# Instance normalization on one core: 24 of 32 units joined in pairs, longer rows for their loads, column halves for their stores

## The chip, the core and the metric

The kernel runs on one core of a Trainium2 chip. The core has five engines that run side by side, each with its own instruction stream: TensorE (PE, matrix products), VectorE (DVE), ScalarE (ACT), GpSimd (POOL) and SyncE (SP). Data move between HBM (the chip's main memory) and SBUF (the on-chip memory with 128 partitions) by 16 DMA engines, which are fed from queues; a queue belongs to the engine that issues the transfer. The metric is the device time of one execution in microseconds (us).

## The reference

```python
B, G, C_per_g, H, W = 4, 8, 16, 256, 256
mu = x.mean(axis=(3, 4), keepdims=True)
var = ((x - mu) ** 2).mean(axis=(3, 4), keepdims=True)
x_norm = (x - mu) / np.sqrt(var + 1e-5)
out = x_norm * gamma[None, :, :, None, None]
```

There are 512 channels of 65,536 float32 numbers. Each is normalized by its own mean and variance and multiplied by its gamma. The input is 134.2 MB and the output as much; both are read or written once.

## The kernel before, in words

The input is cut into `U` = 32 units of 4 MB (16 channels each). A unit lies in SBUF as 128 partitions of `F` = 8192 numbers (32 KB), so that one channel takes `S` = 8 neighbouring partitions. Every partition's row is one run of 32 KB in HBM, and the rows of a unit follow each other without a gap.

There are `AHEAD` = 6 slots of 4 MB in SBUF. `load(u)` brings unit u into slot u % 6. The first six loads are issued at the start: units 1 and 3 by ACT, the others by SP. After that, the load of unit u + 6 stands in the program behind the store of unit u; it is issued by SP, which waits until that store has landed, since it writes the same slot.

For each unit, in order:

- VectorE sums each partition's row (L106) while ScalarE sums the squares (L107, whose elementwise result goes to `junk` and is not used).
- TensorE multiplies the two columns of sums by `navg` (L115), a 128x128 matrix that holds -1/65536 where two partitions belong to one channel. The result `ps` has minus the mean and minus the mean square, already spread over the channel's partitions.
- A short chain makes the scale: `nvar` (L116, VectorE), `std` (L120, ScalarE, a square root), `rstd` (L124, VectorE), and `scale` with gamma's column `g_col` (L126, VectorE).
- VectorE scales the unit in place (L135). For unit 0 ScalarE does the last three eighths (L132).
- ACT issues the store of the unit (L139), and then stands ready for the next unit's squares.

Ahead of the loop, POOL writes a small piece of the output (`touch`), loads gamma and builds `navg`; VectorE repeats gamma eight times along a row (L80), eight small products turn that into columns (L85), and VectorE copies them to `g_col` (L91).

The order of instructions on each engine is the order of the program. Both DMA queues that matter are in this order too: q1 is fed by SP (30 loads), q10 by ACT (2 loads and all 32 stores).

Of the kernel before, what the change touches and what calls it, by code (L numbers as in the profile page):

```python
# [1 line left out]

# [4 lines left out]

F32 = mybir.dt.float32
U8 = mybir.dt.uint8
ALU = mybir.AluOpType  # L10
ACTF = mybir.ActivationFunctionType
AX = mybir.AxisListType


@with_exitstack
def kernel(
    ctx: ExitStack,
    tc: tile.TileContext,
    x: bass.AP,
    gamma: bass.AP,  # L20
    out: bass.AP,
):
    nc = tc.nc
    B, G, C, H, W = x.shape
    P = nc.NUM_PARTITIONS
    HW = H * W
    n_ch = B * G * C
    S = 8
    K = P // S
    F = HW // S  # L30
    U = n_ch // K
    NG = (G * C) // K
    AHEAD = 6
    assert HW % S == 0 and (G * C) % K == 0

    xv = x.rearrange("b g c h w -> (b g c h w)").rearrange("(u p f) -> u p f", p=P, f=F)
    ov = out.rearrange("b g c h w -> (b g c h w)").rearrange("(u p f) -> u p f", p=P, f=F)
    gv = gamma.rearrange("g c -> (g c)")

    data = ctx.enter_context(tc.tile_pool(name="data", bufs=1))  # L40
    singles = ctx.enter_context(tc.tile_pool(name="singles", bufs=1))
    psum = ctx.enter_context(tc.tile_pool(name="psum", bufs=4, space=bass.MemoryType.PSUM))
    ctx.enter_context(tc.manual_schedule())

    slots = [data.tile([P, F], F32, name=f"xt{i}") for i in range(AHEAD)]

    def load(u, queue):
        queue.dma_start(out=slots[u % AHEAD][:], in_=xv[u])  # L48


    g_row = singles.tile([1, G * C], F32, name="g_row")
    touch = singles.tile([16, 128], F32, name="touch")
    nc.vector.memset(touch[:], 0.0)  # L53
    nc.gpsimd.dma_start(out=ov[0][0::S, 0:128], in_=touch[:])  # L54
    nc.gpsimd.dma_start(out=g_row[:], in_=gv[None, :])  # L55
    for u in range(AHEAD):
        load(u, nc.scalar if u in (1, 3) else nc.sync)

    eps_t = singles.tile([P, 1], F32, name="eps_t")
    nc.gpsimd.memset(eps_t[:], 1e-5)  # L60
    one = singles.tile([1, 1], F32, name="one")
    nc.gpsimd.memset(one[:], 1.0)
    navg = singles.tile([P, K, S], F32, name="navg")
    nc.gpsimd.memset(navg[:], -1.0 / HW)  # L64
    nc.gpsimd.affine_select(  # L65
        out=navg[:], in_=navg[:], pattern=[[-S, K], [0, S]], compare_op=ALU.is_ge,
        fill=0.0, base=0, channel_multiplier=1,
    )
    nc.gpsimd.affine_select(  # L69
        out=navg[:], in_=navg[:], pattern=[[S, K], [0, S]], compare_op=ALU.is_ge,  # L70
        fill=0.0, base=S - 1, channel_multiplier=-1,
    )
    navg_w = navg[:].rearrange("p k s -> p (k s)")
    root_eps = singles.tile([P, 1], F32, name="root_eps")
    nc.scalar.activation(out=root_eps[:], in_=eps_t[:], func=ACTF.Sqrt)  # L75
    g_rep = singles.tile([1, NG, K, S], F32, name="g_rep")
    g_ps = psum.tile([P, NG], F32, name="g_ps", bufs=1)
    g_col = singles.tile([P, NG], F32, name="g_col")

    nc.vector.tensor_copy(  # L80
        out=g_rep[:],
        in_=g_row[:].rearrange("o (n k) -> o n k", n=NG).unsqueeze(3).to_broadcast([1, NG, K, S]),
    )
    for n in range(NG):
        nc.tensor.matmul(  # L85
            out=g_ps[:, n : n + 1],
            lhsT=g_rep[:, n].rearrange("o k s -> o (k s)"),
            rhs=one[:],
            start=True, stop=True,
        )  # L90
    nc.vector.tensor_copy(out=g_col[:], in_=g_ps[:])  # L91

    junk = singles.tile([P, F], U8, name="junk")

    st = singles.tile([P, U, 2], F32, name="st")
    nvar = singles.tile([P, U], F32, name="nvar")
    std = singles.tile([P, U], F32, name="std")
    rstd = singles.tile([P, U], F32, name="rstd")
    scale = singles.tile([P, U], F32, name="scale")

    shift = singles.tile([P, 1], F32, name="shift")

    squares = []
    for u in range(U):
        t = slots[u % AHEAD]
        nc.vector.reduce_sum(out=st[:, u, 0:1], in_=t[:], axis=AX.X)  # L106
        square = nc.scalar.activation(  # L107
            out=junk[:], in_=t[:], func=ACTF.Square, accum_out=st[:, u, 1:2],
        )
        if u:  # L110

            tc.declare_no_dep(square.ins, squares[-1].ins, reason="junk, ordered by the root between")
        squares.append(square)
        ps = psum.tile([P, 2], F32, name="ps")
        nc.tensor.matmul(out=ps[:], lhsT=navg_w, rhs=st[:, u], start=True, stop=True)  # L115
        nc.vector.tensor_scalar(  # L116
            out=nvar[:, u : u + 1], in0=ps[:, 0:1], scalar1=ps[:, 0:1],
            scalar2=ps[:, 1:2], op0=ALU.mult, op1=ALU.add,
        )
        nc.scalar.activation(  # L120
            out=std[:, u : u + 1], in_=nvar[:, u : u + 1], func=ACTF.Sqrt,
            bias=eps_t[:], scale=-1.0,
        )
        nc.vector.reciprocal(out=rstd[:, u : u + 1], in_=std[:, u : u + 1])  # L124
        g = u % NG
        nc.vector.tensor_mul(  # L126
            out=scale[:, u : u + 1], in0=rstd[:, u : u + 1], in1=g_col[:, g : g + 1],
        )
        cut = F * 5 // 8 if u == 0 else F
        if cut < F:  # L130
            nc.vector.tensor_mul(out=shift[:], in0=ps[:, 0:1], in1=scale[:, u : u + 1])  # L131
            nc.scalar.activation(  # L132
                out=t[:, cut:], in_=t[:, cut:], func=ACTF.Identity, bias=shift[:], scale=scale[:, u : u + 1],
            )
        nc.vector.tensor_scalar(  # L135
            out=t[:, :cut], in0=t[:, :cut], scalar1=ps[:, 0:1], scalar2=scale[:, u : u + 1],
            op0=ALU.add, op1=ALU.mult,
        )
        nc.scalar.dma_start(out=ov[u], in_=t[:])  # L139
        if u + AHEAD < U:  # L140
            load(u + AHEAD, nc.sync)


# [1 line left out]
_INS = ['x', 'gamma']  # L145
_OUTS = [((4, 8, 16, 256, 256), 'float32')]


# [23 lines left out]
```

## Time and profile before

| | us |
|---|---|
| median of 3 runs | 626.83 (626.78 to 626.91) |
| span of the profiled execution, first to last instruction | 625.2 |
| VectorE busy | 441.8 |
| ScalarE busy | 241.8 |
| TensorE busy | 21.4 |

The trace gives the profiled execution's span; what the timed runs have on top of it is 1.6 us. A row of digits in the profile cuts the span in 40 equal slices and gives the busy share of each in tenths. "DMA" is the mean over the core's 16 DMA engines. A line of the groups names the code line, the engine, the operation, what it writes and reads, the shapes and the count; then the busy time in us and the mean in ns of one; then the engine's idle time just before these instructions and what ended it. "Chain of waits" is the chain of work that ended last, followed back from the last instruction. In it each unit at the start takes VectorE 14.93 us from one reduction to the next.

### The profile page before, as it was taken

How to read it: one execution, taken by the hardware profiler on the slowest of the kernel's cores; microseconds unless marked ns; L12 is line 12 of the kernel's file. 1: busy time of each engine (PE TensorE's matmuls, PEld its weight loads, DVE VectorE, ACT ScalarE, POOL GpSimd, SP SyncE). 2: the span in 40 equal slices, each digit the busy share in tenths (PEclk: the TensorE clock that was granted, in tenths of full speed). 3: DMA queues.
4: the chain of work that ended last, by engine and by line, in shares of the span. 5: the costliest groups of instructions: out<-in, count | busy, mean ns of one | idle time of the engine just before them, and what ended most of it. 6: DMA issues, size and time to landing. Idle time of an engine off the chain costs nothing.

```text
span 625.2 us, 635 instructions
## 1 busy us (share of the span) xinstructions
PE 21.4 (3%) x80; PEld 19.5 (3%) x80; DVE 441.8 (71%) x164; ACT 241.8 (39%) x99; POOL 2.4 (0%) x11
## 2 busy tenths in 40 slices
PE   0200000000000000000000000000000000000000
PEld 0200000000000000000000000000000000000000
DVE  0589999998776687666786767867668676687730
ACT  0464444444443244432344423444224442244400
POOL 1000000000000000000000000000000000000000
DMA  8999999999999999999999999999999999999998
GB/s 370 436 407 432 436 436 436 436 436 430 423 436 434 434 428 434 434 436 436 436 436 428 426 436 436 432 430 434 434 436 436 436 436 421 432 436 434 434 430 367
DMA packets 9282, 268.46 MB, mean 429 GB/s; under 512 B 1072, under 2 KB 1088, under 8 KB 1088
## 3 DMA queue, kind: packets, MB, share of 16 engines
q10 hardware_dynamic: 4896, 142.61, 52.9%
q1 hardware_dynamic: 4320, 125.83, 46.8%
q0 software_dynamic: 64, 0.01, 0.0%
q14 instruction: 2, 0.02, 0.0%
HBM read 134.22 MB, written 134.23 MB: 429 GB/s over the span
## 4 chain that ended last, share of the span: by engine, by line
another core or an unknown queue 61%; DMA 17%; DVE 15%; SPq 1%; PE 1%; issue 0%; ACT 0%
DMA xt<-in_x_dram 10%; DVE st L106 10%; DMA out_dram<-xt 8%; DVE xt L135 5%; SPq L48 1%; PE ps L115 1%; ACT std L120 0%; DVE nvar L116 0%; DVE rstd L124 0%; DVE scale L126 0%; DVE shift L131 0%
## 5 line engine op out<-in xcount | busy, mean ns | idle before, releaser
L106 DVE TENSOR_REDUCE st<-xt 128x1 f32<-128x8192 f32 x32 | 277.9, 8684 | 102.2 <-DMA xt<-in_x_dram 102.2
L107 ACT ACTIVATE junk<-xt 128x8192 uint8<-128x8192 f32 x32 | 225.0, 7030 | 272.0 <-DMA xt<-in_x_dram 233.8
L135 DVE TENSOR_SCALAR xt<-xt,ps,scale 128x8192 f32<-128x8192 f32 (+1 forms) x32 | 144.0, 4500 | 1.1
L120 ACT ACTIVATE std<-nvar,eps_t 128x1 f32<-128x1 f32 x32 | 9.4, 295 | 79.4 <-DVE nvar L116 79.4
L115 PE MATMUL ps<-st,navg 128*128 128x2 f32 x64 | 17.8, 348 | 557.3 <-DVE st L106 557.3
L115 PEld LDWEIGHTS ps<-st,navg 128*128 128x128 f32 x64 | 16.0, 310 | 559.1 <-issue 546.2
L116 DVE TENSOR_SCALAR nvar<-ps 128x1 f32<-128x1 f32 x32 | 9.2, 286 | 23.8 <-PE ps L115 23.8
L124 DVE RECIPROCAL rstd<-std 128x1 f32<-128x1 f32 x32 | 5.2, 163 | 11.6 <-ACT std L120 11.6
L80 DVE COPY g_rep<-g_row 1x1024 f32<-1x1024 f32 x1 | 0.7, 681 | 14.4 <-DMA g_row<-in_gamma_dram 14.4
L107 ACT ACTIVATION_READ_ACCUMULATOR junk<-xt 128x1 f32 x32 | 6.0, 186 | 0.0
L126 DVE TENSOR_TENSOR scale<-rstd,g_col 128x1 f32<-128x1 f32 x32 | 5.1, 158 | 1.1
L85 PE MATMUL g_ps<-one,g_rep 1*128 1x1 f32 x16 | 3.5, 347 | 16.3 <-DVE g_rep L80 16.3
L85 PEld LDWEIGHTS g_ps<-one,g_rep 1*128 1x128 f32 x16 | 3.5, 326 | 16.3 <-issue 16.3
L132 ACT ACTIVATE xt<-xt,shift,scale 128x3072 f32<-128x3072 f32 x1 | 2.9, 2947 | 0.7 <-DVE shift L131 0.7
L91 DVE COPY g_col<-g_ps 128x8 f32<-128x8 f32 x1 | 0.2, 167 | 3.7 <-PE g_ps L85 3.7
L75 ACT ACT_TABLE_LOAD x1 | 1.3, 1283 | 1.7 <-PEq L156 1.7
L53 DVE MEMSET touch<- 16x128 f32 x1 | 0.2, 165 | 0.9 <-PEq L156 0.9
L54 POOL DMA_DIRECT2D out_dram<-touch x1 | 0.6, 617 | 0.8 <-DVE touch L53 0.8
L55 POOL DMA_DIRECT2D g_row<-in_gamma_dram x1 | 0.5, 487 | 0.0
L65 POOL TENSOR_SCALAR_AFFINE_SELECT navg<-navg 128x128 f32<-128x128 f32 x1 | 0.4, 400 | 0.1
L69 POOL TENSOR_SCALAR_AFFINE_SELECT navg<-navg 128x128 f32<-128x128 f32 x1 | 0.4, 399 | 0.1
L64 POOL MEMSET navg<- 128x128 f32 x1 | 0.2, 230 | 0.0
(8 smaller groups left out, 1.0 us busy)
## 6 DMA issues: line engine op xcount, KB each, us to landing
out_dram<-xt ACTq DMA_DIRECT2D x32, 4096.0 KB, 62.5
xt<-in_x_dram SPq DMA_DIRECT2D x30, 4096.0 KB, 38.5
xt<-in_x_dram ACTq DMA_DIRECT2D x2, 4096.0 KB, 31.7
out_dram<-touch POOLq DMA_DIRECT2D x1, 8.0 KB, 9.3
g_row<-in_gamma_dram POOLq DMA_DIRECT2D x1, 0.5 KB, 13.5
```

The costliest lines, as they stand in the source:

```text
L48: queue.dma_start(out=slots[u % AHEAD][:], in_=xv[u])
L75: nc.scalar.activation(out=root_eps[:], in_=eps_t[:], func=ACTF.Sqrt)
L85: nc.tensor.matmul(out=g_ps[:, n : n + 1], lhsT=g_rep[:, n].rearrange("o k s -> o (k s)"), rhs=one[:], start=True, stop=True,)
L106: nc.vector.reduce_sum(out=st[:, u, 0:1], in_=t[:], axis=AX.X)
L107: square = nc.scalar.activation(out=junk[:], in_=t[:], func=ACTF.Square, accum_out=st[:, u, 1:2],)
L115: nc.tensor.matmul(out=ps[:], lhsT=navg_w, rhs=st[:, u], start=True, stop=True)
L116: nc.vector.tensor_scalar(out=nvar[:, u : u + 1], in0=ps[:, 0:1], scalar1=ps[:, 0:1], scalar2=ps[:, 1:2], op0=ALU.mult, op1=ALU.add,)
L120: nc.scalar.activation(out=std[:, u : u + 1], in_=nvar[:, u : u + 1], func=ACTF.Sqrt, bias=eps_t[:], scale=-1.0,)
L124: nc.vector.reciprocal(out=rstd[:, u : u + 1], in_=std[:, u : u + 1])
L126: nc.vector.tensor_mul(out=scale[:, u : u + 1], in0=rstd[:, u : u + 1], in1=g_col[:, g : g + 1],)
L132: nc.scalar.activation(out=t[:, cut:], in_=t[:, cut:], func=ACTF.Identity, bias=shift[:], scale=scale[:, u : u + 1],)
L135: nc.vector.tensor_scalar(out=t[:, :cut], in0=t[:, :cut], scalar1=ps[:, 0:1], scalar2=scale[:, u : u + 1], op0=ALU.add, op1=ALU.mult,)
```

## The change

24 of the 32 units (4 to 27) are joined in pairs to twelve units of 8 MB. A joined unit has 32 channels, a channel takes 4 partitions (`S` = 4), and a partition's row is one run of 64 KB in HBM. It is loaded by one DMA. It is stored by two, one for each half of the columns: rows of 32 KB that step 64 KB in HBM. The first four and the last four units stay at 4 MB. In the order of units there are now 20: four single, twelve joined, four single.

The six slots become three tiles of 8 MB; a single unit takes one half of such a tile, a joined unit a whole one. The first five loads (four single units, one joined) are issued at the start. A later load is issued when the stores of all data that it overwrites have landed, so a joined one waits for two stores.

The reductions and squares keep their shape, 128 x 8192, so a joined unit has two of each; two products accumulate in one `ps`, and there is one short chain for the whole unit. The scaling is done half by half, and each half's store is issued as soon as it is scaled. `navg` and `g_col` are made twice, for S = 8 and S = 4.

```diff
-    S = 8
-    AHEAD = 6
+    HALVES = 6
+    ENDS = 4
+    sizes = [1] * ENDS + [2] * ((n_half - 2 * ENDS) // 2) + [1] * ENDS
+    starts = [sum(sizes[:i]) for i in range(len(sizes))]
...
+    def rows(flat, u):
+        n = sizes[u] * P * F
+        lo = starts[u] * P * F
+        return flat[lo : lo + n].rearrange("(p f) -> p f", p=P)
...
-    slots = [data.tile([P, F], F32, name=f"xt{i}") for i in range(AHEAD)]
+    pairs = [data.tile([P, 2 * F], F32, name=f"xt{i}") for i in range(HALVES // 2)]
+
+    def home(u):
+        at = starts[u] % HALVES
+        return pairs[at // 2], (at % 2) * F
 
     def load(u, queue):
-        queue.dma_start(out=slots[u % AHEAD][:], in_=xv[u])
+        t, c = home(u)
+        src = rows(x_flat, u)
+        n = sizes[u] * F
+        step = n
+        for k in range(0, n, step):
+            queue.dma_start(out=t[:, c + k : c + k + step], in_=src[:, k : k + step])
...
-    for u in range(AHEAD):
+    first = [u for u in range(len(sizes)) if starts[u] + sizes[u] <= HALVES]
+    for u in first:
         load(u, nc.scalar if u in (1, 3) else nc.sync)
...
+    for S in (8, 4):
...
     for u in range(U):
-        t = slots[u % AHEAD]
-        nc.vector.reduce_sum(out=st[:, u, 0:1], in_=t[:], axis=AX.X)
-        square = nc.scalar.activation(
-            out=junk[:], in_=t[:], func=ACTF.Square, accum_out=st[:, u, 1:2],
-        )
+        t, c = home(u)
+        S = 8 // sizes[u]
+        halves = range(sizes[u])
+        for h in halves:
+            part = t[:, c + h * F : c + (h + 1) * F]
+            col = starts[u] + h
+            nc.vector.reduce_sum(out=st[:, col, 0:1], in_=part, axis=AX.X)
+            square = nc.scalar.activation(
+                out=junk[:], in_=part, func=ACTF.Square, accum_out=st[:, col, 1:2],
+            )
...
-        nc.tensor.matmul(out=ps[:], lhsT=navg_w, rhs=st[:, u], start=True, stop=True)
+        for h in halves:
+            nc.tensor.matmul(
+                out=ps[:], lhsT=navg[S], rhs=st[:, starts[u] + h],
+                start=h == 0, stop=h == sizes[u] - 1,
+            )
...
-        nc.vector.tensor_scalar(
-            out=t[:, :cut], in0=t[:, :cut], scalar1=ps[:, 0:1], scalar2=scale[:, u : u + 1],
-            op0=ALU.add, op1=ALU.mult,
-        )
-        nc.scalar.dma_start(out=ov[u], in_=t[:])
-        if u + AHEAD < U:
-            load(u + AHEAD, nc.sync)
+        dst = rows(o_flat, u)
+        step = F
+        for k in range(0, sizes[u] * F, step):
+            n = min(step, cut - k)
+            nc.vector.tensor_scalar(
+                out=t[:, c + k : c + k + n], in0=t[:, c + k : c + k + n], scalar1=ps[:, 0:1],
+                scalar2=scale[:, u : u + 1], op0=ALU.add, op1=ALU.mult,
+            )
+            nc.scalar.dma_start(out=dst[:, k : k + step], in_=t[:, c + k : c + k + step])
+
+        for v in range(len(first), U):
+            need = starts[v] + sizes[v] - HALVES
+            if starts[u] < need <= starts[u] + sizes[u]:
+                load(v, nc.sync)
```

More of the change, by code (lines that the diff above doesn't have):

```diff
@@ L26 @@
     HW = H * W
-    n_ch = B * G * C
-    S = 8
[L29 to L32, printed above, removed]
-    AHEAD = 6
-    assert HW % S == 0 and (G * C) % K == 0
-    xv = x.rearrange("b g c h w -> (b g c h w)").rearrange("(u p f) -> u p f", p=P, f=F)
-    ov = out.rearrange("b g c h w -> (b g c h w)").rearrange("(u p f) -> u p f", p=P, f=F)
+    F = 8192
+    HALVES = 6
+    n_half = (B * G * C * HW) // (P * F)
+    ENDS = 4
+    assert n_half * P * F == B * G * C * HW and HW % (2 * F) == 0
+    sizes = [1] * ENDS + [2] * ((n_half - 2 * ENDS) // 2) + [1] * ENDS
+    starts = [sum(sizes[:i]) for i in range(len(sizes))]
+    assert sum(sizes) == n_half
+    xf = x.rearrange("b g c h w -> (b g c h w)")
+    of = out.rearrange("b g c h w -> (b g c h w)")
     gv = gamma.rearrange("g c -> (g c)")
+    def rows(flat, u):
+        n = sizes[u] * P * F
+        lo = starts[u] * P * F
+        return flat[lo : lo + n].rearrange("(p f) -> p f", p=P)
     data = ctx.enter_context(tc.tile_pool(name="data", bufs=1))
@@ L43 @@
     ctx.enter_context(tc.manual_schedule())
-    slots = [data.tile([P, F], F32, name=f"xt{i}") for i in range(AHEAD)]
+    pairs = [data.tile([P, 2 * F], F32, name=f"xt{i}") for i in range(HALVES // 2)]
+    def home(u):
+        at = starts[u] % HALVES
+        return pairs[at // 2], (at % 2) * F
     def load(u, queue):
-        queue.dma_start(out=slots[u % AHEAD][:], in_=xv[u])
+        t, c = home(u)
[4 more added lines that the diff above has]
+            queue.dma_start(out=t[:, c + k : c + k + step], in_=src[:, k : k + step])
+    x_flat, o_flat = xf, of
     g_row = singles.tile([1, G * C], F32, name="g_row")
@@ L53 @@
     nc.vector.memset(touch[:], 0.0)
-    nc.gpsimd.dma_start(out=ov[0][0::S, 0:128], in_=touch[:])
+    nc.gpsimd.dma_start(out=rows(o_flat, 0)[0::8, 0:128], in_=touch[:])
     nc.gpsimd.dma_start(out=g_row[:], in_=gv[None, :])
-    for u in range(AHEAD):
+    first = [u for u in range(len(sizes)) if starts[u] + sizes[u] <= HALVES]
+    for u in first:
         load(u, nc.scalar if u in (1, 3) else nc.sync)
@@ L62 @@
     nc.gpsimd.memset(one[:], 1.0)
[L63 to L67, printed above, removed]
-    )
-    nc.gpsimd.affine_select(
-        out=navg[:], in_=navg[:], pattern=[[S, K], [0, S]], compare_op=ALU.is_ge,
-        fill=0.0, base=S - 1, channel_multiplier=-1,
-    )
-    navg_w = navg[:].rearrange("p k s -> p (k s)")
+    navg, g_col = {}, {}
@@ new lines @@
+    for S in (8, 4):
+        K = P // S
+        w = singles.tile([P, K, S], F32, name=f"navg{S}")
+        nc.gpsimd.memset(w[:], -1.0 / HW)
+        nc.gpsimd.affine_select(
+            out=w[:], in_=w[:], pattern=[[-S, K], [0, S]], compare_op=ALU.is_ge,
+            fill=0.0, base=0, channel_multiplier=1,
+        )
+        nc.gpsimd.affine_select(
+            out=w[:], in_=w[:], pattern=[[S, K], [0, S]], compare_op=ALU.is_ge,
+            fill=0.0, base=S - 1, channel_multiplier=-1,
+        )
+        navg[S] = w[:].rearrange("p k s -> p (k s)")
@@ L74 @@
     root_eps = singles.tile([P, 1], F32, name="root_eps")
     nc.scalar.activation(out=root_eps[:], in_=eps_t[:], func=ACTF.Sqrt)
[L76 to L89, printed above, removed]
-        )
@@ L91 @@
-    nc.vector.tensor_copy(out=g_col[:], in_=g_ps[:])
+    g_all = singles.tile([1, G * C * 8], F32, name="g_all")
+    for S in (8, 4):
+        K = P // S
+        n_g = (G * C) // K
+        g_rep = g_all[:, : G * C * S].rearrange("o (c s) -> o c s", s=S)
+        nc.vector.tensor_copy(
+            out=g_rep, in_=g_row[:].unsqueeze(2).to_broadcast([1, G * C, S]),
+        )
+        g_ps = psum.tile([P, n_g], F32, name=f"g_ps{S}", bufs=1)
+        g_col[S] = singles.tile([P, n_g], F32, name=f"g_col{S}")
+        for n in range(n_g):
+            nc.tensor.matmul(
+                out=g_ps[:, n : n + 1],
+                lhsT=g_all[:, n * P : (n + 1) * P],
+                rhs=one[:],
+                start=True, stop=True,
+            )
+        nc.vector.tensor_copy(out=g_col[S][:], in_=g_ps[:])
@@ L93 @@
     junk = singles.tile([P, F], U8, name="junk")
-    st = singles.tile([P, U, 2], F32, name="st")
+    U = len(sizes)
+    st = singles.tile([P, n_half, 2], F32, name="st")
     nvar = singles.tile([P, U], F32, name="nvar")
@@ L104 @@
     for u in range(U):
-        t = slots[u % AHEAD]
-        nc.vector.reduce_sum(out=st[:, u, 0:1], in_=t[:], axis=AX.X)
-        square = nc.scalar.activation(
-            out=junk[:], in_=t[:], func=ACTF.Square, accum_out=st[:, u, 1:2],
[L109 to L113, printed above, removed]
-        ps = psum.tile([P, 2], F32, name="ps")
-        nc.tensor.matmul(out=ps[:], lhsT=navg_w, rhs=st[:, u], start=True, stop=True)
+        t, c = home(u)
[7 more added lines that the diff above has]
+                out=junk[:], in_=part, func=ACTF.Square, accum_out=st[:, col, 1:2],
+            )
+            if squares and h == 0:
+                tc.declare_no_dep(square.ins, squares[-1].ins, reason="junk, ordered by the root between")
+            squares.append(square)
+        ps = psum.tile([P, 2], F32, name="ps")
+        for h in halves:
+            nc.tensor.matmul(
+                out=ps[:], lhsT=navg[S], rhs=st[:, starts[u] + h],
+                start=h == 0, stop=h == sizes[u] - 1,
+            )
         nc.vector.tensor_scalar(
```

14 lines of the change are left out of this document (8 added, 6 removed).

## The prediction

> **What bounds the kernel now.** I read the head of the page first, with its busy rows and its queue table.
>
> ```profile
> span 625.2 us, 635 instructions
> ...
> PE 21.4 (3%) x80; PEld 19.5 (3%) x80; DVE 441.8 (71%) x164; ACT 241.8 (39%) x99; POOL 2.4 (0%) x11
> ...
> DVE  0589999998776687666786767867668676687730
> ...
> DMA  8999999999999999999999999999999999999998
> ...
> q10 hardware_dynamic: 4896, 142.61, 52.9%
> q1 hardware_dynamic: 4320, 125.83, 46.8%
> ```
>
> No compute engine is full, but the two DMA queues together fill 52.9 + 46.8 = 99.7% of the time of all 16 DMA engines. The stretch view, asked for the middle of the run, says the same: DMA share 1.00 (the last but one number), at 433 GB/s.
>
> ```profile
> 110.00:540.00 430.00, 12.81 (x46) 11.50 (x46) 316.53 (x116) 170.60 (x69) 0.00 (x0) 1.00 1.00 433
> ```
>
> So the time is 268.46 MB at some 433 GB/s (620 us), plus about 1.8 us before the first byte, 1 to 2 us after the last, and little else. The waits of the SP queue (what, on what: us in total, times, longest) and the page's list of DMA issues (last number: us from issue to landing) show why no engine starves: loads wait for stores to free a slot, and stores stand in a line three deep (62.5 us to land, where 4.19 MB at 433 GB/s need 9.7 us alone and 19.4 us at half rate).
>
> ```profile
> SPq L48 <- DMA out_dram<-xt: 514.7, 26, 39.7
> ```
>
> ```profile
> out_dram<-xt ACTq DMA_DIRECT2D x32, 4096.0 KB, 62.5
> xt<-in_x_dram SPq DMA_DIRECT2D x30, 4096.0 KB, 38.5
> ```
>
> Last, the groups of instructions, for the durations:
>
> ```profile
> L106 DVE TENSOR_REDUCE st<-xt 128x1 f32<-128x8192 f32 x32 | 277.9, 8684 | 102.2 <-DMA xt<-in_x_dram 102.2
> L135 DVE TENSOR_SCALAR xt<-xt,ps,scale 128x8192 f32<-128x8192 f32 (+1 forms) x32 | 144.0, 4500 | 1.1
> L80 DVE COPY g_rep<-g_row 1x1024 f32<-1x1024 f32 x1 | 0.7, 681 | 14.4 <-DMA g_row<-in_gamma_dram 14.4
> L91 DVE COPY g_col<-g_ps 128x8 f32<-128x8 f32 x1 | 0.2, 167 | 3.7 <-PE g_ps L85 3.7
> ```
>
> VectorE idles 102.2 us ahead of its reductions, waiting for loads. It follows the DMAs, and its work is worth nothing unless it gets late enough to empty both queues.
>
> **The change, part by part.**
>
> *Fewer and longer packets.* In the queue table a packet is one row, plus one 4-byte semaphore write per DMA and engine: q1 has 30 loads x (128 + 16) = 4320. The change turns 24 x 128 = 3072 load rows of 32 KB into 1536 of 64 KB, so each of the 16 engines handles 96 fewer packets. The bytes stay. What is saved is the fixed cost of a packet, and no row shows a 64 KB packet. Its bounds come from the trace's packet records: 32 KB packets take 1213 ns nearly throughout, the 4-byte ones 9 ns. A packet that carries almost nothing bounds the fixed cost: 0 to 9 ns, so 96 packets save 0 to 0.86 us. I take the middle, 4.5 ns: 0.43 us. I do not reckon below nothing here, because a 64 KB row is the same run of bytes in both memories; a dearer row is the second rival.
>
> A rule of the Trainium skill ("DMA: Bandwidth & Descriptors", "Why small descriptors are slow") gives some 3 cycles a packet inside a DMA engine. At that page's 850 MHz this is 3.5 ns, an estimate by which the sum would be 0.34 us instead of 0.43.
>
> *Fewer DMAs.* 32 loads become 20, the stores stay 32: 12 fewer semaphore writes per engine at 9 ns, 0.11 us. Twelve issues on SP (0.33 us each in the chain of waits) go too, worth nothing: store packets keep the engines busy meanwhile.
>
> *Stores.* Same 32, same 32 KB rows, but 24 of them step 64 KB between rows in HBM. No row has that step. I take no cost, as the nearest row is the present store at a step of 32 KB, whose packets take the same 1213 ns as the loads'. The other end is in the second rival.
>
> *Compute per unit.* A joined unit has two reductions, then one chain instead of two, then two scalings: 2 x 8.68 + 0.57 x 2 (PE, now two accumulated products) + about 1.4 (nvar, std, rstd, scale and their gaps) + 2 x 4.55 = 29.0 us, against 2 x 14.93 = 29.9 us for two units in the chain of waits. ACT needs 2 x (7.03 + 0.19) us for its squares beside the 17.4 us of reductions. Gained on VectorE: 0.9 us per pair; on the path: nothing.
>
> *What gets coarser.* The first half of a joined unit waits for all 8 MB to land, and a load of 8 MB waits for two stores. This costs DMA time only where both queues are empty. Steady state: a pair takes the DMAs 16.78 MB / 433 GB/s = 38.7 us and VectorE 29.0, so VectorE never has a second pair waiting, and of three slots two are left to the queues. Margin 9.7 us per pair.
>
> *The start,* where VectorE is full (the 9s of its row), is the tight place. Put the work in a line, each 4.19 MB being 9.7 us. Six loaded units fill the DMAs from 1.8 to 59.9 us. The first four stores are issued at 36.5, 51.2, 66.1 and about 81 us, as now. The joined load behind them is issued when stores 0 and 1 have landed; since nothing stands idle, that is by 59.9 + 19.4 = 79.3 us. By then store 2 is queued, which lasts until 89.0: margin 9.7 us. With store 3 the work lasts to 98.7, with the joined load to 118. The first joined unit's first half is scaled at about 81 + 17.4 + 2.5 + 4.55 = 105.5 us: margin 12.5 us. No sharing between the queues enters here, so it holds even if 64 KB load packets alternating with 32 KB store packets take two thirds of the rate. I expect them to.
>
> *Preparation.* A second gamma column is made ahead of unit 0: one more copy to 1x512 (half of 0.681 us), four products for eight (half of 3.54 us), a copy of 0.17: 2.3 us behind 20.06 us, so 22.4, just ahead of the first landing at 22.77. At the full price of the first column (4.6 us) it delays VectorE by 1.9 us, inside the 9.7 above: nothing. Three more POOL instructions end near 5 us, unseen.
>
> *The end.* Single units again. The last store now goes at 600.6 us, and stores queued ahead of it run until 623.9 - 9.7 = 614. Nothing moves unless it is issued 13 us late.
>
> **Sum.** -0.43 - 0.11 = -0.54 us on a span of 625.2 us. The trace gives the profiled execution no time but its span; the timed runs of 626.78 to 626.91 lie 1.6 us above it, which I keep. 624.7 + 1.6 = 626.3 us against the median of 626.83. A difference under 0.2% (1.25 us) is about what a measurement here can't tell from no change.
>
> **Rivals.**
>
> *Rows split again.* If a 64 KB row goes out as two packets of 32 KB, only the semaphores are saved: 626.7 us. No row speaks for or against. 0.08, inside 0.2%.
>
> *Strided rows are dearer, so it is slower.* The 24 store halves that step 64 KB are 24 x 8 = 192 packets per engine, 233 us of its time at 1.213 us. Each per cent on them costs 2.3 us; 0.8% (1.8 us, with the 0.54 saved) already makes it slower than the bound. The price goes by the packet records: 99 in 100 of q10's packets took at most 1228 ns, 1.2% over the usual; if every strided one took that, 2.9 us are added: 629.2 us. The far end is the slowest record, about 2.0 us for the first packet of a queue, which at 192 packets would be 151 us. Against: both queues run at the same packet time now, so HBM is not what limits them, and the slow records stand alone. For: no row has this step. I give 0.13. The Trainium skill ("DMA: Bandwidth & Descriptors", "Latency and other measured facts") has row pitches of 512 KiB at 207 GB/s against 214 when padded, which on these stores would be an estimated 7.9 us, 634.2 us; that pitch is eight times the one here, and no run shows either.
>
> *A queue runs dry.* If whole-pair landing makes VectorE or the slots later than the 9.7 us at the start, each further microsecond is lost in full; at 15 us late, 5.3 us: 631.6 us. For: coarser slots. Against: the margins above. 0.09.
>
> *Packets cost more than their records say, so it is faster than the bound.* 96 fewer packets must save over 12 ns each (with the semaphores' 0.11 us). 20 ns would give 1.9 + 0.1 us: 624.8 us. Against: 9 ns for an all but empty one. 0.11. Beside it the Trainium skill ("DMA: Bandwidth & Descriptors", "Where 436 GB/s comes from") puts the ceiling of the ports at 435 GB/s, against 433 here; that leaves little for anything.
>
> **How the numbers follow.** My forecast has 0.59, and with split rows 0.67 lies within 0.2%. Slower is 0.13 + 0.09 = 0.22, faster 0.11. The range goes down to 625.0, which takes in both ends of the packet cost (625.9) and the larger part of the fast case. It goes up to 630.0, over stores dearer by up to 1.6% and a dry spell of 3 us. About 0.05 lies below and 0.1 above.
>
> **What would show it.** q1 should have 18 loads x 144 = 2592 packets (4128 if rows are split), q10 still 4896, their shares together 99.7%, the GB/s row steady at 433 to 434 in the middle. VectorE's idle time ahead of its reductions should gather in fewer, longer waits. A DMA digit under 9 near 79 to 118 us, or at one place of every 38.7 us, would say the slots are too coarse; a full DMA row with under 430 GB/s would say that rows got dearer; over 435 GB/s, that packets were worth more than I gave them.

## The result, and the profile after

The changed kernel takes 629.71 us in the median (628.85 to 629.88, five runs) against 626.83 us before (626.78 to 627.34): a ratio of 1.0039, with a 95% interval from 1.0026 to 1.0051. It is slower by some 2.9 us, where I had forecast 0.5 us less. The profiled execution took 629.86 us with a span of 628.15 us, 2.9 us more than before.

The head of the page after, first:

```profile
span 628.2 us, 584 instructions
...
DVE  0689998593966929669396793958939489997800
...
DMA  8999999999999999999999999999999999999997
...
q10 hardware_dynamic: 4896, 142.61, 52.7%
q1 hardware_dynamic: 2592, 125.83, 46.7%
q8 instruction: 1, 0.02, 0.0%
```

q1 has the 2592 packets that whole 64 KB rows make. The q8 row, one transfer of instructions, is not on the page before; it matters at the end. The two queues still fill 99.4% of the DMA engines' time, now of a longer span. So the engines do not stand idle more; they were busy longer with the same bytes. The middle stretch is as fast as before, at 433 GB/s:

```profile
110.00:540.00 430.00, 12.28 (x44) 11.03 (x44) 303.26 (x78) 166.87 (x56) 0.00 (x0) 1.00 1.00 433
```

The waits of SP and the issues (as before: last number, us from issue to landing; joined loads are the third line):

```profile
SPq L64 <- DMA out_dram<-xt: 547.0, 16, 69.7
```

```profile
out_dram<-xt ACTq DMA_DIRECT2D x32, 4096.0 KB, 44.3
xt<-in_x_dram SPq DMA_DIRECT2D x6, 4096.0 KB, 27.2
xt<-in_x_dram SPq DMA_DIRECT2D x12, 33.2
```

A joined load lands 33.2 us after its issue, where 4 MB took 38.5 us before, because its long packets get two thirds of the rate and because it finds its queue empty. The longest wait of SP has grown to 69.7 us: the first reload, unit 5, waits that long for store 0, and then for store 1. SP issues it at 81.3 us:

```profile
81.34 41.47 SPq L64 DMA_DIRECT2D xt<-in_x_dram  x2
```

By the packet records the last packet of the first loads had ended at 70.0 us, and the first packet of this reload starts at 85.8 us. For 15.8 us the load queue was empty, while stores kept all engines busy. Just there the time is lost. These are the stretches from 75 to 105 us, before and then after (last number: GB/s):

```profile
75.00:105.00 30.00, 1.26 (x6) 1.14 (x6) 27.50 (x10) 14.83 (x6) 0.00 (x0) 1.00 1.00 429
```

```profile
75.00:105.00 30.00, 1.22 (x5) 1.02 (x5) 28.25 (x11) 14.84 (x6) 0.00 (x0) 1.00 1.01 412
```

The engines' share is full in both, but 412 GB/s instead of 429 means that (1 - 412/429) x 30 = 1.2 us of work is missing. In the packet records, sixteen store packets that start from 84.2 us on take 1456 to 1899 ns instead of 1213, the reload's first one on each engine 3065 to 4280 ns instead of 2418, and the second on ten of them 2607 to 2968 ns. After that, packets take their usual times again, but for single ones.

The packet records give a full account of the span. "Usual" is 1213 ns for 32 KB and 2418 ns for 64 KB; the first three rows are means over the 16 DMA engines:

| us | before | after | difference |
|---|---|---|---|
| packets of loads and stores at their usual times | 621.06 | 620.29 | -0.77 |
| what single packets took beyond that | 1.56 | 3.49 | +1.93 |
| gaps and semaphore writes, less the overlap of the records, until an engine's last store | 0.70 | 1.07 | +0.37 |
| the last engine behind the mean one, at the end | 0.61 | 1.73 | +1.12 |
| from there to the end of the span | 1.31 | 1.57 | +0.26 |
| span | 625.24 | 628.15 | +2.91 |

The first and the third row belong together. A record overlaps the next one on its engine by some 4 ns, and each engine has 96 records fewer, so most of the +0.37 is overlap that is missing. Together the two rows save 0.40 us.

So there are two losses. The larger one is slow packets: 1.93 us. Of the excess, 2.34 us (0.16 before) come after 60 us, 1.8 of them in packets that start between 84 and 92 us.

The other loss is the last engine, which ends 1.73 us behind the mean, 1.12 us more than before. Most of it has nothing to do with the slow packets. The engine that ends last is the one that carried the q8 row: 16 KB of instructions at 595.0 us, which took 931 ns, and the store packet behind it took 399 ns more than usual. Every engine is busy to the end, so it never catches up. The next engine ends 0.72 us earlier, at 625.87 us instead of 626.59. In the kernel before, this transfer comes at 625.6 us, behind the last store, and delays nothing. Why it comes earlier now was not found. The rest of the 1.12 us, 0.4, is what the slow packets and other small delays left unequal.

### The profile page after: what moved, and what is told of

It reads as the page before. It is cut to its first block, busy times and chain, and to the rows that moved or that the text cites. A ratio compares the mean times of both kernels' runs of the same rounds, so it can differ in the third digit from the quotient of the medians.

```text
span 628.2 us, 584 instructions
## 1 busy us (share of the span) xinstructions
PE 23.3 (4%) x88; PEld 21.3 (3%) x88; DVE 433.0 (69%) x130; ACT 238.2 (38%) x87; POOL 3.6 (1%) x14
## 3 DMA queue, kind: packets, MB, share of 16 engines
q1 hardware_dynamic: 2592, 125.83, 46.7%
## 4 chain that ended last, share of the span: by engine, by line
another core or an unknown queue 52%; DMA 27%; DVE 14%; PE 1%; SPq 1%; issue 0%; ACT 0%
DMA out_dram<-xt 14%; DMA xt<-in_x_dram 13%; DVE st L135 10%; DVE xt L173 4%; PE ps L144 1%; SPq L64 1%; ACT std L152 0%; DVE nvar L148 0%; DVE rstd L156 0%; DVE scale L159 0%; DVE shift L164 0%
## 5 line engine op out<-in xcount | busy, mean ns | idle before, releaser
L152 ACT ACTIVATE std<-nvar,eps_t 128x1 f32<-128x1 f32 x20 | 5.9, 294 | 66.4 <-DVE nvar L148 66.4
L148 DVE TENSOR_SCALAR nvar<-ps 128x1 f32<-128x1 f32 x20 | 5.7, 287 | 14.9 <-PE ps L144 14.9
L156 DVE RECIPROCAL rstd<-std 128x1 f32<-128x1 f32 x20 | 3.3, 164 | 7.2 <-ACT std L152 7.2
L109 PE MATMUL g_ps<-one,g_all 1*128 1x1 f32 x24 | 5.4, 348 | 16.6 <-DVE g_all L103 16.6
L109 PEld LDWEIGHTS g_ps<-one,g_all 1*128 1x128 f32 x24 | 5.3, 324 | 16.6 <-issue 15.9
L159 DVE TENSOR_TENSOR scale<-rstd,g_col 128x1 f32<-128x1 f32 x20 | 3.2, 159 | 0.7
## 6 DMA issues: line engine op xcount, KB each, us to landing
xt<-in_x_dram SPq DMA_DIRECT2D x12, 33.2
```

What stands on the lines that cost most here:

```text
L109: nc.tensor.matmul(out=g_ps[:, n : n + 1], lhsT=g_all[:, n * P : (n + 1) * P], rhs=one[:], start=True, stop=True,)
L148: nc.vector.tensor_scalar(out=nvar[:, u : u + 1], in0=ps[:, 0:1], scalar1=ps[:, 0:1], scalar2=ps[:, 1:2], op0=ALU.mult, op1=ALU.add,)
L152: nc.scalar.activation(out=std[:, u : u + 1], in_=nvar[:, u : u + 1], func=ACTF.Sqrt, bias=eps_t[:], scale=-1.0,)
L159: nc.vector.tensor_mul(out=scale[:, u : u + 1], in0=rstd[:, u : u + 1], in1=g_col[S][:, g : g + 1],)
```

## Experiments

Each is an edit of the changed kernel or of the kernel before. In every one that names times of packets, these are from the packet records of its profile. A table of all of them stands at the end of this section. The runs are from several chips, so ratios are compared, each against the kernel before on the same chip.

**Half loads.** The joined units stay, with loads in two column halves:

```diff
         n = sizes[u] * F
-        step = n
+        step = F
```

> The changed kernel, but a joined unit is loaded by two DMAs, one for each half of the columns, so all packets have 32 KB; slots, waits and stores stay. In the profile of the changed kernel the load queue q1 stood empty from about 70 to 86 us of the span, and from 84 to 92 us the packets of both queues were slow (1.9 us more per DMA engine than their usual 2418 and 1213 ns, unevenly over the engines). Theory 'dry and cold' (the first reload after the load queue has run dry in the start stalls the DMA engines): with equal shares the six first loads end near 80 us and the reload is still issued near 81 us, so the queue is dry for some 5 us, and a stall of about 1.5 to 3 us stays: 628 to 629.5 us. Theory 'long rows' (packets of 64 KB stall when they meet other traffic in the start): no stall, no slow packets, 626.5 to 627.2 us. Theory 'collision' (the reload on SP is issued within half a microsecond of a store on ACT, at 81.3 and 81.1 us): the stall stays if the reload is still issued at 81 us, 628 to 629.5 us.

It took 627.76 us (ratio 1.0010, interval 1.0000 to 1.0020). Its load queue did not run dry: the first half of a reload waits for one store only, so it was issued long before the queue was empty, and there were no slow packets after 60 us beyond 0.21 us. From 75 to 105 us it moved 429 GB/s:

```profile
75.00:105.00 30.00, 1.34 (x6) 1.14 (x5) 28.12 (x11) 14.84 (x6) 0.00 (x0) 1.00 0.99 429
```

Most of the loss is gone, but this run changed the rows and the waiting together.

**Eight single ends.**

```diff
-    ENDS = 4
+    ENDS = 8
```

> The changed kernel with eight single units at each end instead of four, so sixteen units are joined to eight. The six first loads are single, and the first reloads are single units behind one store each, so the load queue does not run dry in the start. 'Dry and cold': no stall near 84 us, 626.2 to 627 us. 'Long rows': a stall moves to the first joined load near 100 to 120 us, 628 to 630 us. 'Collision': none is to be expected, 626.2 to 627 us.

629.19 us (1.0031, 1.0020 to 1.0043). The slow packets moved to the first joined load, as "long rows" said: 1.27 us per engine on its packets, from 124.5 us on. But I had overlooked that the load queue runs dry there too, from 118.9 us, since that load is the first to wait for two stores. The run does not tell the two apart.

**The kernel before with paired loads, twice.**

```diff
-        nc.scalar.dma_start(out=ov[u], in_=t[:])
-        if u + AHEAD < U:
-            load(u + AHEAD, nc.sync)
+        store = nc.scalar.dma_start(out=ov[u], in_=t[:])
+        if u % 2 and u - 1 + AHEAD < U:
+            early = load(u - 1 + AHEAD, nc.sync)
+            tc.add_manual_dep(early.ins, store.ins.name, ...)
+            load(u + AHEAD, nc.sync)
```

> The kernel before (all units 4 MB, rows of 32 KB), but its reloads are issued in pairs: the loads of units u+5 and u+6 both wait for the store of the odd unit u. So the first reload comes at about 81 us, when the load queue has just run dry (about 80 us), near the issue of a store on ACT (81 us), and without any row of 64 KB. 'Dry and cold' and 'collision': slow packets from 84 us on and 628 to 629.5 us. 'Long rows': none, 626.6 to 627.4 us.

629.12 us (1.0035, 1.0014 to 1.0057; one of ten executions took 635.4 us). Its profiled execution, the fastest of them with 627.8 us, had no slow packets after 60 us (0.10 us), though the queue was empty from 80.5 to 85.9. So I looked at one more.

> The kernel before with its reloads in pairs, profiled once more. The last profile of it (627.8 us, the lowest of ten executions; the others lay mostly at 628.4 to 629.4) showed the load queue empty from 80.5 to 85.9 us and no slow packet behind that. 'Dry and cold': a usual execution near 629 us has slow packets when the queue starts again near 86 us, worth 1 to 2 us. 'Long rows': none there either, as all rows have 32 KB, and what the other executions lose lies elsewhere.

This execution took 629.12 us, and has the slow packets: 1.68 us per engine after 60 us, the first in the stores from 84 us on. All its rows have 32 KB, and nothing is joined. The stretch from 75 to 105 us of the faster profile and then of this one:

```profile
75.00:105.00 30.00, 1.26 (x6) 1.14 (x6) 27.51 (x10) 14.83 (x6) 0.00 (x0) 1.00 1.01 435
```

```profile
75.00:105.00 30.00, 1.25 (x6) 1.14 (x5) 27.51 (x10) 14.83 (x6) 0.00 (x0) 1.00 1.00 411
```

The two executions are of one program, and their mean DMA engines end 1.23 us apart (623.56 and 624.79 us). Long rows are not needed for the loss; waiting for two stores is enough. That it is so in most executions is only inferred, from their times.

**Half loads, dry.** The half loads, whose first half now waits for both stores:

```diff
+            if stores and k == 0 and n > step:
+                tc.add_manual_dep(got.ins, stores[starts[u] + 1 - HALVES].ins.name, ...)
```

> The changed kernel with joined units loaded as two column halves (rows of 32 KB), and the first half now waits for both stores, as a whole joined load does. The load queue then runs dry near 80 us and starts again near 85 us, with 32 KB rows. Before this wait the same kernel took 627.8 us in the median and showed no slow packets after 44 us. 'Dry and cold': slow packets near 85 us, 628.5 to 630 us. 'Long rows': none, 627.3 to 628.2 us.

629.66 us (1.0037, 1.0023 to 1.0051), against a ratio of 1.0010 (1.0000 to 1.0020) without this one wait. The queue is empty from 80.0 to 86.5 us, slow packets cost 1.62 us per engine after 60 us, and the last engine ends 1.79 us behind the mean. This is the cleanest pair: same rows, same DMAs, same compute. The mean engine ends 1.41 us later (624.76 against 623.35 us); the last engines differ by more, but in both profiles the last one is that of the late instruction transfer.

```profile
75.00:105.00 30.00, 1.34 (x6) 1.14 (x5) 28.13 (x11) 14.84 (x6) 0.00 (x0) 1.00 1.01 416
```

**Late first reload.** The reload of unit 5 also waits for the first reduction of unit 4:

```diff
+            total = nc.vector.reduce_sum(out=st[:, col, 0:1], in_=part, axis=AX.X)
+            if u == 4 and h == 0:
+                late = load(5, nc.sync)
+                tc.add_manual_dep(late.ins, total.ins.name, ...)
+                load(6, nc.sync)
```

> The changed kernel, but the first reload (unit 5) also waits for the first reduction of unit 4, so it is issued near 89.5 us instead of 81.3, with no store issued on ACT between 81 and 105 us. The stores already queued keep the DMA engines busy until about 100 us. 'Collision': no stall, 626.5 to 627 us. 'Dry and cold' and 'long rows': the slow packets move to about 92 to 100 us, 628.5 to 630 us.

629.3 us (1.0035, 1.0022 to 1.0048). The slow packets moved with the reload: they start from 92.7 to 95.7 us (1.99 us after 60 us), with no store issued near them. "Collision" falls.

**Small load first.**

```diff
+            if u == 3:
+                small = nc.sync.dma_start(out=spare[:], in_=gv[None, :])
+                tc.add_manual_dep(small.ins, total.ins.name, ...)
+                load(5, nc.sync)
```

> The changed kernel with one more DMA on SP: gamma (512 bytes) into a spare tile, issued behind the first reduction of unit 3 (74.4 us), when the load queue is empty, and ahead of the first reload at 81.3 us. 'Dry and cold': this small load takes the first restart of the queue, so the slow packets move to about 78 us or vanish, and the first reload's packets take their usual 2418 ns; 626.3 to 628.5 us. 'Long rows': the first reload's packets stay slow near 85 us, 628.5 to 630 us.

629.46 us (1.0039, 1.0025 to 1.0052). The small load was issued at 74.7 us, and the first reload's packets were slow all the same (1.96 us after 60 us). A load that one DMA engine carries does not take the restart's cost away.

**Filled queue.**

```diff
+    for v in range(len(sizes) - 3, len(sizes)):
+        nc.sync.dma_start(out=rows(o_flat, v), in_=rows(x_flat, v))
```

> The changed kernel with three copies of 4 MB from input to output in HBM queued on SP behind the first loads (for the last three units, whose output is stored again at the end), so that the load queue is never empty until the first reload of 64 KB rows is behind them. They add 3 x 9.7 us of DMA time, so about 655 us without a stall. 'Dry and cold': the first reload's packets take their usual 2418 ns, about 655 to 656 us. 'Long rows': the first reload's packets are slow all the same, about 657 to 659 us.

659.21 us, one execution. The first reload, 64 KB rows behind a queue that had not run dry, started at 119.5 us with 0.05 us of excess. But the copies themselves ran beside the stores with slow packets (most of the 3.38 us after 60 us), so its total says nothing. The restart at 157 us, after the first dry spell, was free (0.02 us): a first restart is not always slow.

**Dry in the middle.** The kernel before, with reloads 17 to 19 behind the third of their stores, and 25 to 27 likewise:

```diff
-        if u + AHEAD < U:
+        if u + AHEAD < U and u not in (11, 12, 13, 19, 20, 21):
             load(u + AHEAD, nc.sync)
+        if u in (13, 21):
+            early = load(u - 2 + AHEAD, nc.sync)
+            tc.add_manual_dep(early.ins, store.ins.name, ...)
+            load(u - 1 + AHEAD, nc.sync)
+            load(u + AHEAD, nc.sync)
```

> The kernel before, unchanged in its start, but twice in the middle (units 11 to 13 and 19 to 21) three reloads together wait for the third of their stores, so that the load queue runs dry near 280 and near 435 us, with 32 KB rows, while three stores are queued. In the runs so far only the first restart after a dry spell stalled, always within the first 130 us; later restarts of the same kernels took no extra time. 'First restart' (whenever it comes, it stalls, and leaves the DMA engines out of step): slow packets at the first dry spell, near 290 us, little at the second, 628.3 to 629.5 us. 'Only in the start' (something that is over after some 130 us): no slow packets in either, 626.8 to 627.5 us. If both restarts stall, the count of restarts does not matter, but what is in flight at them.

629.89 us (1.0044, 1.0027 to 1.0061). The first dry spell lasted from 293.7 to 308.4 us. No packet was slow at its restart, and packets that started ten us later lost 0.2 us per engine. The second did not come about. The time was lost otherwise: the last loads came so late that no DMA engine had work for 3.1 us near 615 us. Without that it would be 626.8 us, as before.

**Out of step first.**

```diff
+    last = len(sizes) - 1
+    nc.sync.dma_start(out=rows(o_flat, last)[0:8, 0:4096], in_=rows(x_flat, last)[0:8, 0:4096])
```

> The changed kernel with a small copy in HBM (8 rows of 16 KB, for the last unit, whose output is stored again at the end) on SP behind the first loads. It runs on 8 of the 16 DMA engines near 70 us and delays these by some 0.6 us, half a packet. 'In step' (the restart stalls because all 16 engines start their loads within a microsecond; afterwards they are out of step and later restarts are free): the slow packets at the first reload near 85 us shrink to under half, 627 to 628.5 us. 'First restart' for another reason: the stall stays, 629.5 to 630.5 us with the 0.6 us of the copy.

629.67 us (1.0041, 1.0026 to 1.0056). Eight engines were held for 611 ns each at 70.6 us; the reload behind still had 1.72 us of excess on its packets. That half a packet of offset protects the restart is refuted.

**Join from 12, join from 16.**

```diff
-    sizes = [1] * ENDS + [2] * ((n_half - 2 * ENDS) // 2) + [1] * ENDS
+    sizes = [1] * 12 + [2] * ((n_half - 12 - ENDS) // 2) + [1] * ENDS
```

(and the same with 16).

> The changed kernel with the first twelve units single, then eight joined units, then four single ones. The load queue runs dry for the first time near 195 us, behind the last single reload, and then at every joined one (10 us each). 'First restart' (the first restart stalls, whenever it comes): slow packets near 200 us, 628.5 to 630 us. 'Only in the start' (as the dry spells at 294 us of the last run suggest, whose restart took 0.2 us): no slow packets but those near 41 us, 626.3 to 627.3 us.

> As join_from_12, with the first sixteen units single and six joined ones; the first dry spell comes near 275 us. 'First restart': slow packets near 280 us, 628.5 to 630 us. 'Only in the start': none, 626.5 to 627.4 us, and its packets of 64 KB save half of the 0.4 us that all twelve joined loads would.

628.61 us (1.0023, 1.0013 to 1.0032) and 629.05 us (1.0031, 1.0020 to 1.0041). In both the first restart is slow, at 203 and 280 us, though by less (0.63 and 0.43 us on the reload's packets). "Only in the start" falls too, as a rule. The engines drift apart here for another reason as well. In the first of the two runs the last engine ends a store 0.3 us behind the mean for store 4, but 1.1 us for stores 5 to 7, ahead of the dry spell: 8 KB of instructions had held one engine at 141.9 us.

The table: when the load queue was first empty, the excess of packets after 60 us, and how far the last engine ended behind the mean. In eight of the ten programs that are built on the changed kernel, itself among them, that last engine is the one that carried 16 KB of instructions between 592 and 606 us (not in late first reload and filled queue). In those built on the kernel before, this transfer comes behind the last store.

| run | rows of loads | first empty, us | excess | last engine | median us | ratio |
|---|---|---|---|---|---|---|
| before | 32 KB | only behind the last load | 0.16 | 0.61 | 626.83 | 1 |
| half loads | 32 KB | only behind the last load | 0.21 | 1.21 | 627.76 | 1.0010 |
| paired, first profile | 32 KB | 80.5 to 85.9 | 0.10 | 0.75 | 629.12 | 1.0035 |
| paired, second profile | 32 KB | 80.0 to 86.5 | 1.68 | 0.83 | 629.12 | one run |
| half loads, dry | 32 KB | 80.0 to 86.5 | 1.62 | 1.79 | 629.66 | 1.0037 |
| after | 64 KB | 70.0 to 85.8 | 2.34 | 1.73 | 629.71 | 1.0039 |
| late first reload | 64 KB | 70.1 to 94.3 | 1.99 | 0.78 | 629.30 | 1.0035 |
| small load first | 64 KB | 70.3 to 86.1, but for the small load | 1.96 | 1.77 | 629.46 | 1.0039 |
| out of step first | 64 KB | 71.6 to 86.0 | 2.18 | 1.22 | 629.67 | 1.0041 |
| filled queue | 64 KB | 148.3 to 157.2 | 3.38 | 1.18 | 659.21 | one run |
| eight single ends | 64 KB | 118.9 to 124.5 | 1.89 | 1.15 | 629.19 | 1.0031 |
| join from 12 | 64 KB | 197.2 to 203.1 | 1.01 | 1.73 | 628.61 | 1.0023 |
| join from 16 | 64 KB | 274.7 to 280.3 | 1.14 | 1.67 | 629.05 | 1.0031 |
| dry in the middle | 32 KB | 293.7 to 308.4 | 0.67 | 0.09 | 629.89 | 1.0044 |

## Why the prediction was wrong

**What held.** The kernel is bound by its DMA engines, and stays so. The packet count of q1 is 2592, as forecast. The packet term came out as well: from the start of a packet to the start of the next one behind it on its engine, 32 KB take 1209.4 ns and 64 KB 2414.1 in the mean, so a joined row saves 4.7 ns, and 96 of them 0.45 us, where I had 0.43. That it hits so well is luck: 4.5 ns was the middle of bounds from 0 to 9. Store rows that step 64 KB cost nothing: between 120 and 520 us the median packet of q10 takes 1213 ns in both kernels, the mean 1214.0 ns against 1213.4. The Trainium skill's row pitch rule ("DMA: Bandwidth & Descriptors", "Latency and other measured facts") starts at eight times this pitch, and the trace shows nothing of it here (its 214 GB/s, which the prediction uses, is for a padded pitch of 4 MiB). Two thirds of the rate for the long packets came out (291 of 434 GB/s for q1 from 46 to 68 us, by the packet records). The first reload was issued at 81.3 us, 2 us behind the bound of 79.3, which leaves out the slow packets of the first 46 us (1.15 us). The first joined store was issued at 104.3 us (105.5 forecast), and no DMA engine ran out of work for as long as 1 us.

**The step that failed** is the sentence on what gets coarser: "This costs DMA time only where both queues are empty." The margins worked out from it, 9.7 and 12.5 us, were about right, and they measured the wrong thing. It is enough that the load queue alone runs empty. When it starts again for the first time, the packets of both queues are slow for some microseconds, in most runs, though the engines are never without work: 1.78 us per engine in the changed kernel, against a forecast gain of 0.54. I could have seen the dry spell coming: with two thirds of the rate from 41 us on, the 8 MB of unit 4 end near 70 us, and I had its successor's issue at 79. I took that for harmless, because I priced idle engines and nothing else.

The trace before had a warning that I misread. The prediction says that the slow records stand alone and that the slowest one, 2.0 us, is the first packet of a queue. In fact 28 packets with such records stand together, from 39.9 to 42.0 us, where the first store joins the loads. They cost 0.8 us per engine, and the slowest record, a load's, is one of them. All 14 profiles have such a group there, of 0.6 to 1.1 us, and no queue had run dry before it. So packets can be slow where one direction of traffic joins the other, also without a dry spell.

**A second gap** was to treat the 16 engines as one. The mean engine ended 1.53 us later, but the kernel ends with the slowest engine, and that added 1.12 us. Some 0.7 us of it is the instruction transfer that now comes ahead of the last stores, of which the prediction has no word; the rest is unequal delays.

**The rivals.** "A queue runs dry" named the right place, but charged the time in which both queues are empty; by that price the change was still free. "Strided rows are dearer" gave 629.2 us, close to the measured time and for a reason that the packets refute. "Packets cost more than their records say" fails by the 4.7 ns. Split rows did not occur. The range of 625.0 to 630.0 us held the time, but for the sake of these rivals; the sign was wrong.

**What stays open.** That a first restart of the load queue is slow, in most runs, was shown with 32 KB and with 64 KB rows, and removed by taking away one wait. Why it is slow was not found, nor whether the slow group at 41 us has the same cause. A simultaneous issue on ACT is excluded, and neither half a packet of offset nor a small load ahead avoids it. It varies between executions (0.00 and 1.56 us at the restart in two profiles of one kernel), and tends to be smaller later in the run (1.78 us at 86 us in the changed kernel, 1.40 at 124.5, 0.73 at 203, 0.45 at 280, none at 157 in filled queue and at 308 in dry in the middle). Later restarts of the same run are nearly free. Whether 64 KB rows in a queue that never runs dry would gain their 0.45 us was not measured: with three tiles of 8 MB a joined reload always has to wait for two stores. The half loads are still 0.6 us above the kernel before in the runs beside them. In their profile the mean engine ends as before (623.35 against 623.33 us), and the last one 1.21 us behind it instead of 0.61; it is the one with the late instruction transfer. No version here beats the kernel before.

## What to carry to other kernels

In a kernel that is bound by its DMA engines, look not only at whether some queue has work but at whether each direction's queue keeps some: a coarser slot that makes a load wait for two stores can empty the load queue while every engine is busy, and here that cost about four times what fewer packets and DMAs were to bring. Work out when each queue ends under the real sharing, which went by packet here, so that longer rows on one side drained that side sooner. And let the end be set by the slowest of the DMA engines, not by their mean: look in the trace for what else that engine carried.

## What the runs showed of the hardware

- Packets followed each other on an engine every 607 ns for 16 KB, 1209.4 for 32 KB and 2414.1 for 64 KB, so 4.6 to 4.7 ns of a packet did not grow with its size. The records themselves are some 4 ns longer (611, 1213 and 2418 ns) and overlap.
- Two busy queues alternated by packets, not by bytes: 64 KB packets beside 32 KB packets got 291 of 434 GB/s.
- A load queue that had run dry took its first packet about 3.3 us after SP's issue in the steady state (161.1 to 164.5 us), and 4.5 us at the first restart; the other queue covers that.
- The first restart after a dry spell slowed the packets of both queues, by 0.4 to 1.8 us per engine, in all but three of the profiles in the table that have a dry spell (paired, first profile; dry in the middle; filled queue). Where the first store joined the loads, near 41 us, all 14 profiles lost 0.6 to 1.1 us per engine.
- Instructions travel on the same DMA engines as the data: 16 KB took 931 ns of one engine at 595.0 us in the changed kernel and made the next packet 399 ns longer; 8 KB took 309 ns, with 536 and 252 ns on the next packet (before, at 143.9 and 199.4 us). As the engines are never idle here, that engine stayed behind.
